# All eight triangular inverses in one chain, the last four heads in the order q, k, v, z, the input in four loads, the bias product as a whole tile, and new slots

## The chip, the cores and the metric

The kernel runs on one core of a Trainium2 chip. Its engines each work through a queue of their own in order: TensorE (PE, with its weight loads PEld), VectorE (DVE), ScalarE (ACT), GpSimd (POOL) and SyncE (SP, which only issues DMAs here). The metric is the device time of one execution, in microseconds, as a median of runs.

## What is computed

One decoder layer for 256 positions of width 1024, in float32:

```python
h = rms_norm(x, norm_w)
q_a, k_a, v_a, z_a, qkv_dn, z_dn, b_dn, a_dn = split(h @ w_in)
qa, ka = rms_norm(heads(q_a)), rms_norm(heads(k_a))     # 8 heads of 64
y_a = softmax(qa ka^T / 8 + rel_bias, causal) va * silu(z_a)
q, k, v = silu(causal_conv4(qkv_dn))                    # 4 heads of 128, q and k L2-normed
# chunks of 64: amat = I + strict(beta k k^T decay); u, w = solve(amat, ...)
o_d = delta_rule(q, k, v, decay, beta)
y_d = rms_norm(o_d) * silu(z_dn)
out = x + concat(y_a, y_d) @ w_out
```

With 256 positions the block-sparse attention has one block, so it is plain causal attention.

## The kernel before

**Products.** A float32 product is made from rounded halves: each weight chunk is copied to a high half (ScalarE, L195) and the rest (VectorE, L196), x and y likewise, and each product takes three matmuls of 256 (or 264) columns: L256 to L258 (`gemm`), L747 to L749 (`dn`), L836 to L838 (`oproj`). There are 960 of these in the program: z (gates, 96), d (delta rule's q, k, v, 288), a (attention, 384) and o (output, 192). I number them from 0 and say "product 792" for the place where o02, the first output chunk, ends. The chunks come in the order z0 to z7, d0 to d11, a (per half of the heads v, q, k, z) and o. The weights and x come by SP's queue (L183, L208): x is eight loads, one per 128 rows of the width, each followed by one z chunk.

**Order.** TensorE's order is written by hand: `products()` yields after groups of six products, and each yield is one step (`advance`). Other work of TensorE sits in generators (streams): `norm`, `gates`, `bias`, `prep0` and `prep2` (two delta-rule heads each), `heads` (norm and transpose of q and k), `pair0` to `pair3` (attention of two heads), `base` with `levels` (the triangular inverses) and `scan0` to `scan3` (the delta rule of one head). Each goes on with its next stage at the step that the table AT gives, or later if a condition in it isn't met. What a step issues stands in TensorE's queue behind the products yielded so far. The other engines are ordered by the scheduler.

**Inverses.** The 256 positions of a head are taken in two chunks of 128 (which gives the same as four of 64), so there are eight matrices of 128 by 128. `base(gq)` inverts 16 by 16 blocks of four of them by a recurrence of 15 steps with two VectorE instructions each (L507, L509); it is started after prep0 (gq 0) and after prep2 (gq 1). `levels` then joins 16 to 32, 64 and 128 by small matmuls (L529 on), each followed by a copy out of the bank on ScalarE or VectorE; when a chain is done it starts its two scans. A scan makes v (L589, L593), the state and output of its first part (L595, L596), the second part's products with the state (L610, L611), L618, L622, and then the norm, the gate (L630) and the transposes (L634), from which yh and yl (L635, L636) are made.

**Output.** OUTS gives the order of the output chunks: o02, o00, o12, o10, o03, o13, o01, o11. A chunk with second digit 2 needs heads 0 to 3 of the attention, 0 scans 0 and 1, 3 heads 4 to 7, 1 scans 2 and 3. The steps between the last product of o02 and the first of o00 hold all that is still missing for scans 0 and 1. The first split row of the output that depends on them is yl. At the end VectorE adds the residual and the result is stored.

**Bias.** Row 0 to 32 of T hold a one-hot table, `rbt` the bias values; one matmul (L381) makes the eight rows, which go by ScalarE (L384) and DRAM back into T.

Of the kernel before, what the change touches and what calls it, by code (L numbers as in the profile page):

```python
# [14 lines left out]
P = 128  # L15
# [22 lines left out]
    ("attention", 0): 88, ("attention", 1): 97, ("attention", 2): 128, ("attention", 3): 117, ("attention", 4): 120,  # L38
# [3 lines left out]
    ("base1", 8): 124, ("bias", 0): 0, ("bias", 1): 6, ("bias", 2): 43, ("gates", 0): 29, ("gates", 1): 35,  # L42
# [13 lines left out]
}  # L56
SEGS = (2, 0, 1, 3)
# [4 lines left out]
def tile_hymba_layer(ctx: ExitStack, tc: tile.TileContext, xt, wz, wdn, wat, wout, rb, cst, oneh, out):  # L62
# [81 lines left out]
    rbt = new([33, 8], "rbt")  # L144
    oht = T.rearrange("p h s -> p (h s)")[0:33, 0:384]
    POOL.memset(rbt, NEG)
    nc.gpsimd.dma_start(rbt[0:32, :], rb)
    nc.gpsimd.dma_start(oht, oneh)
    for _ in range(NWARM):
# [14 lines left out]
              + [(f"a{s}{i}", wat[4 * s + i], 1024) for hf in range(2) for s in SEGS for i in (2 * hf, 2 * hf + 1)]  # L164
# [40 lines left out]

    for k in range(KT):
        r = slice(P_COLS + k * S if k else 0, P_COLS + (k + 1) * S)
        nc.sync.dma_start(px[:, r], xt[:, r])  # L208
        load()
# [28 lines left out]
    Mts = [new([P, 4, 32], f"Mt{g}") for g in range(2)]  # L238
# [3 lines left out]
    def basis():  # L242
        for t in Mts:
            nc.gpsimd.dma_start(t, cst[:, C_ND, :])
# [178 lines left out]
    def prep(hp, n, ps):  # L423
# [50 lines left out]
        start(f"base{hp // 2}", base(hp // 2))  # L474
# [12 lines left out]
    def base(gq):  # L487
        us = slice(4 * gq, 4 * gq + 4)
        pk = rot([P, 16, 4], f"pk{gq}", "pk")
        for q in range(4):  # L490
            r = slice(32 * q, 32 * q + 32)

            DVE.scalar_tensor_tensor(out=pk[r].rearrange("p i u -> p u i"), in0=LT[r, us, 32 * q + 16:32 * q + 32],
                                     scalar=cs2[r, 0:1], in1=LT[r, us, 32 * q:32 * q + 16], op0=ALU.mult, op1=ALU.add)
        Lb = rot([P, 16, 32], f"Lb{gq}", "Lb", 1)
        DVE.transpose(Lb, pk.unsqueeze(3).to_broadcast([P, 16, 4, 8]))
        Mt = Mts[gq]
        tm = rot([P, 4, 16], f"tm{gq}", "tm")
# [4 lines left out]
        for r in range(15):  # L503
            w, nc_ = 15 - r, r // 8 + 1
            t = ap(tm, 0, (32, 2), (16, nc_), (1, w))
            m = ap(Mt, r + 1, (80, 2), (32, nc_), (1, w))
            SUB.tensor_tensor(out=t, in0=ap(Lb, 32 * (r + 1) + r, (16, 2), (0, nc_), (32, w)),  # L507
                               in1=ap(Mt, r, (80, 2), (32, nc_), (0, w)), op=ALU.mult)
            SUB.tensor_tensor(out=m, in0=m, in1=t, op=ALU.subtract)  # L509

        Mp = rot([P, 4, 4, 8], f"Mp{gq}", "Mp")
        DVE.transpose(Mp.rearrange("p u c g -> p c u g"), Mt)
        Mp = Mp.rearrange("p u c g -> p u (c g)")
        for q in range(4):
            r = slice(32 * q, 32 * q + 32)
            DVE.transpose(MT[r, us, r], Mp[r])
        yield W_BASE
        yield from levels(gq, Mp)


    def levels(gq, Mp):
# [25 lines left out]
        for q in range(2):  # L547
            POOL.tensor_copy(M[qs[q], us, qs[q]], Mp[qs[q]])
# [387 lines left out]
```

## Time and profile before

| | us |
|---|---|
| median of 3 runs | 166.14 (164.9 to 166.62) |
| profiled run | 166.0 |
| span of its trace | 164.1 |
| TensorE busy (share of the span) | 156.8 (96%) |
| VectorE busy | 130.3 (79%) |
| ScalarE busy | 103.1 (63%) |

The busy share is an average over stages. Matmuls are pipelined, so a row's duration is longer than the distance to the next row; what a matmul costs is that distance. A bracket at a row's end is the idle time before it and what ended it.

### The profile page before, as it was taken

The page shows a single profiled execution, that of the slowest core. Times are in us where ns is not written, and L with a number is a line of the kernel's source. Part 1 is how long each engine was busy: PE and PEld are TensorE (multiplying, and loading weights), DVE is VectorE, ACT ScalarE, POOL GpSimd, SP SyncE. Part 2 cuts the span into 40 slices and gives each one's busy share as a digit, 9 for nine tenths or more (in the row PEclk, how much of TensorE's full clock was granted, in tenths as well). Part 3 has the DMA queues.
Part 4 walks back from the last instruction along what each step waited for, and adds up shares of the span by engine and source line. Part 5 has one row for each costly group of instructions (what it writes and reads, how often), then busy time and mean ns, then how long its engine had stood idle before and what let it go on. Part 6 is the DMA issues. An engine that isn't in the chain of part 4 may idle for free.

```text
span 164.1 us, 4034 instructions
## 1 busy us (share of the span) xinstructions
PE 156.8 (96%) x1548; PEld 148.3 (90%) x1548; DVE 130.3 (79%) x381; ACT 103.1 (63%) x244; POOL 19.8 (12%) x29
## 2 busy tenths in 40 slices
PE   7999899999999999999999999999999979999990
PEld 7869899999999999999999989989988858999990
DVE  2569859999598999999999999987676997356261
ACT  5769497539988558787636695655657885343100
POOL 7200410000002000031230001042220010003000
PEclk9999999999999999999999999999999999999999
DMA  5999888899965327574344434434312300000033
GB/s 148 270 365 355 248 262 222 248 179 192 339 206 209 128 80 213 223 216 172 122 138 135 132 123 134 128 132 132 116 51 93 128 0 4 0 0 0 4 128 128
DMA packets 9930, 25.01 MB, mean 152 GB/s; under 512 B 1165, under 2 KB 3981, under 8 KB 9912
## 3 DMA queue, kind: packets, MB, share of 16 engines
q1 hardware_dynamic: 9208, 23.66, 46.6%
q10 hardware_dynamic: 576, 0.92, 1.5%
q8 instruction: 12, 0.20, 0.5%
q0 software_dynamic: 128, 0.18, 0.4%
q14 instruction: 6, 0.05, 0.1%
HBM read 23.52 MB, written 1.25 MB: 151 GB/s over the span
## 4 chain that ended last, share of the span: by engine, by line
PE 70%; DVE 13%; ACT 6%; DMA 3%; issue 2%; SPq 2%; POOL 1%; DVEq 0%
PE ps L256 8%; PE ps L257 7%; PE ps L258 7%; PE ps L748 6%; PE ps L749 6%; PE ps L747 6%; PE ps L836 4%; PE ps L838 4%; PE ps L837 4%; DVE wl_d L196 3%; DMA px<-xt 3%; PE ps L462 2%; DVE cv L407 2%; PE ps L689 1%; PE ps L712 1%
## 5 line engine op out<-in xcount | busy, mean ns | idle before, releaser
L256 PE MATMUL ps<-wh_a,xh 128*128 128x256 f32 x96 | 28.5, 297 | 0.0
L747 PE MATMUL ps<-xh,wh_d 128*128 128x256 f32 x96 | 27.8, 289 | 0.0
L748 PE MATMUL ps<-xl,wh_d 128*128 128x256 f32 x96 | 26.8, 280 | 0.0
L749 PE MATMUL ps<-xh,wl_d 128*128 128x256 f32 x96 | 26.8, 279 | 0.0
L257 PE MATMUL ps<-wh_a,xl 128*128 128x256 f32 x96 | 26.7, 279 | 0.0
L258 PE MATMUL ps<-wl_a,xh 128*128 128x256 f32 x96 | 26.7, 279 | 0.0
L195 ACT CAST wh_a<-wr_a 128x1024 fp32r<-128x1024 f32 x16 | 16.8, 1049 | 7.2 <-PE ps L748 3.7
L196 DVE TENSOR_TENSOR wl_a<-wr_a,wh_a 128x1024 fp32r<-128x1024 f32 x16 | 19.4, 1215 | 0.7 <-ACT wh_a L195 0.6
L256 PEld LDWEIGHTS ps<-wh_a,xh 128*128 128x128 f32 x96 | 18.1, 188 | 0.7 <-issue 0.5
L836 PE MATMUL ps<-yh,wh_o 128*128 128x256 f32 x64 | 18.7, 292 | 0.0
L257 PEld LDWEIGHTS ps<-wh_a,xl 128*128 128x128 f32 x96 | 18.1, 188 | 0.1
L258 PEld LDWEIGHTS ps<-wl_a,xh 128*128 128x128 f32 x96 | 18.1, 189 | 0.0
L748 PEld LDWEIGHTS ps<-xl,wh_d 128*128 128x128 f32 x96 | 18.1, 188 | 0.1
L747 PEld LDWEIGHTS ps<-xh,wh_d 128*128 128x128 f32 x96 | 18.0, 188 | 0.1
L407 DVE SCALAR_TENSOR_TENSOR cv<-un,px,cv 128x255 f32<-128x255 f32 (+2 forms) x36 | 16.4, 475 | 2.0 <-ACT cv L405 2.0
L749 PEld LDWEIGHTS ps<-xh,wl_d 128*128 128x128 f32 x96 | 18.0, 187 | 0.0
L837 PE MATMUL ps<-yl,wh_o 128*128 128x256 f32 x64 | 17.9, 280 | 0.0
L838 PE MATMUL ps<-yh,wl_o 128*128 128x256 f32 x64 | 17.9, 279 | 0.0
L196 DVE TENSOR_TENSOR wl_d<-wr_d,wh_d 128x1024 fp32r<-128x1024 f32 x12 | 14.6, 1214 | 1.2 <-ACT wh_d L195 1.1
L195 ACT CAST wh_d<-wr_d 128x1024 fp32r<-128x1024 f32 x12 | 12.6, 1052 | 2.4 <-PE ps L748 1.9
L196 DVE TENSOR_TENSOR wl_o<-wr_o,wh_o 128x1024 fp32r<-128x1024 f32 x8 | 9.8, 1221 | 3.6 <-ACT wh_o L195 3.6
L836 PEld LDWEIGHTS ps<-yh,wh_o 128*128 128x128 f32 x64 | 12.0, 188 | 0.5 <-issue 0.3
(210 smaller groups left out, 406.7 us busy)
## 6 DMA issues: line engine op xcount, KB each, us to landing
wr_a<-wat SPq DMA_DIRECT2D x16, 512.0 KB, 3.3
wr_d<-wdn SPq DMA_DIRECT2D x12, 512.0 KB, 5.6
wr_o<-wout SPq DMA_DIRECT2D x8, 512.0 KB, 3.3
wr_z<-wz SPq DMA_DIRECT2D x7, 260.0 KB, 5.8
T<-bd SPq DMA_DIRECT2D x8, 128.0 KB, 5.8
px<-xt SPq DMA_DIRECT2D x7, 128.0 KB, 4.9
out_t<-ot ACTq DMA_DIRECT2D x3, 256.0 KB, 2.4
cs<-cst SPq DMA_DIRECT2D x1, 192.0 KB, 4.9
```

The lines of the kernel that those rows point to most:

```text
L195: ACT.copy(h[:, r], raw[:, r])
L196: eng.tensor_tensor(out=l[:, r], in0=raw[:, r], in1=h[:, r].bitcast(F32), op=ALU.subtract)
L256: PE.matmul(ps, lhsT=xa, rhs=wh[:, cols], start=first, stop=False)
L257: PE.matmul(ps, lhsT=xb, rhs=wh[:, cols], start=False, stop=False)
L258: PE.matmul(ps, lhsT=xa, rhs=wl[:, cols], start=False, stop=last)
L407: DVE.scalar_tensor_tensor(out=a[:, 3 - j:], in0=src[:, 0:S - 3 + j], scalar=pr[:, o + j:o + j + 1], in1=a[:, 3 - j:], op0=ALU.mult, op1=A ...
L747: PE.matmul(ps, lhsT=w[0][:, wk], rhs=xh[:, k, :], start=first, stop=False)
L748: PE.matmul(ps, lhsT=w[0][:, wk], rhs=xl[:, k, :], start=False, stop=False)
L749: PE.matmul(ps, lhsT=w[1][:, wk], rhs=xh[:, k, :], start=False, stop=last)
L836: PE.matmul(ps, lhsT=w[0][:, o], rhs=yh[:, k, :], start=(first and j == 0 and (m % 2 == 0 or alone)), stop=False)
L837: PE.matmul(ps, lhsT=w[0][:, o], rhs=yl[:, k, :], start=False, stop=False)
L838: PE.matmul(ps, lhsT=w[1][:, o], rhs=yh[:, k, :], start=False, stop=(last and j == 1 and (m % 2 == 1 or alone)))
```

## The change

**Inverses.** There is one `base()` and one `levels()` for all eight, started in prep2 only. The 15 steps work on twice the width, so there are 30 VectorE instructions instead of 60; the basis tile is one `Mt` of 320 columns. `levels` takes two banks. The last copy is split: VectorE takes heads 0 and 1 (L579), ScalarE the others. All four scans are started together at the end.

**Attention.** The half for the last four heads is projected as q, k, v, z instead of v, q, k, z. **Input.** x comes in four loads of two slices. **Bias.** `rbt` and the one-hot table are parts of T, filled up to 128 rows with zeros, and the matmul writes 128 rows of 384. **Slots.** The table AT is new throughout; code lines of after are 2 or 3 higher.

```diff
-SEGS = (2, 0, 1, 3)
+SEGS = ((2, 0), (0, 0), (1, 0), (3, 0), (0, 1), (1, 1), (2, 1), (3, 1))
...
+    Tf = T.rearrange("p h s -> p (h s)")
+    oht, rbt = Tf[:, 0:384], Tf[:, 384:512]
+    POOL.memset(Tf[:, 0:512], 0.0)
...
-        nc.sync.dma_start(px[:, r], xt[:, r])
+        if k % 2 == 0:
+            r = slice(P_COLS + k * S if k else 0, P_COLS + (k + 2) * S)
+            nc.sync.dma_start(px[:, r], xt[:, r])
         load()
...
-        PE.matmul(b[0:8, :384], lhsT=rbt, rhs=oht, start=True, stop=True)
+        PE.matmul(b[:, :384], lhsT=rbt, rhs=oht, start=True, stop=True)
...
-        start(f"base{hp // 2}", base(hp // 2))
+        if hp == 2:
+            start("base", base())
...
-            t = ap(tm, 0, (32, 2), (16, nc_), (1, w))
+            t = ap(tm, 0, (32, 4), (16, nc_), (1, w))
...
-        ACT.mul(MT[0:64, us, 64:128], b64[0:64, 0], -1.0)
-        free.append(b)
-        yield W_LV
-        start(f"scan{2 * gq}", scan(2 * gq))
-        yield 1
-        start(f"scan{2 * gq + 1}", scan(2 * gq + 1))
+        DVE.tensor_scalar(out=MT[0:64, 0:4, 64:128], in0=b64[0:64, 0:4], scalar1=-1.0, scalar2=None, op0=ALU.mult)
+        ACT.mul(MT[0:64, 4:8, 64:128], b64[0:64, 4:8], -1.0)
+        free.extend((ba, bb))
+        for h in range(DH):
+            start(f"scan{h}", scan(h))
...
-        while done["vz"] < 2 + 2 * (pa // 2):
+        while (2, pa // 2) not in done or (3, pa // 2) not in done:
```

ScalarE at the start of the program, before (xh is the high half of x, sq the squares for the norm, wh_z the high half of a z chunk):

```order
L266 ACTIVATE xh<-px 128x256
L123 ACTIVATE eal<-px 128x4
L195 CAST wh_z_165<-wr_z_99 128x256
L195 CAST wh_z_165<-wr_z_99 128x264
L276 ACTIVATE sq_296<-px 128x512
L266 ACTIVATE xh<-px 128x256
L195 CAST wh_z_171<-wr_z_99 128x520
```

and of the change:

```order
L278 ACTIVATE sq_277<-px 128x512
L268 ACTIVATE xh<-px 128x256 x2
L121 ACTIVATE eal<-px 128x4
L195 CAST wh_z_160<-wr_z_99 128x256
L195 CAST wh_z_160<-wr_z_99 128x264
L195 CAST wh_z_166<-wr_z_99 128x520
```

A pass of squares and a second pass of xh now stand ahead of the first wh_z.

TensorE inside o02 (wh_o and wl_o are the halves of its weights), of the change; in before these products have only one transpose, L634 of scan 1, between them:

```order
L840 MATMUL ps_72<-yh,wl_o_1532 128x256
L578 MATMUL ps_77<-MT,X_1851 32x64 x16
L838 MATMUL ps_75<-yh,wh_o_1531 128x256
L839 MATMUL ps_75<-yl,wh_o_1531 128x256
L840 MATMUL ps_75<-yh,wl_o_1532 128x256
L838 MATMUL ps_75<-yh,wh_o_1531 128x256
L839 MATMUL ps_75<-yl,wh_o_1531 128x256
L840 MATMUL ps_75<-yh,wl_o_1532 128x256
L592 MATMUL ps_73<-vt,MT 128x128
L592 MATMUL ps_71<-vt,MT 128x128
```

The last step of the inverses (L578) and the first step of scans 0 and 1 (L592) now stand among o02's products, six products apart; L562 to L564 and L572 stand ahead of them in the same way.

TensorE between o02 and o00, before (S is a scan's state, pb the softmax weights, yd a scan's output):

```order
L838 MATMUL ps_74<-yh,wl_o_1704 128x256
L610 MATMUL ps_72<-S_1883,kq_134 128x128
L611 MATMUL ps_72<-S_1883,kq_134 128x128
L589 MATMUL ps_78<-vt,MT 128x128
```

and of the change:

```order
L840 MATMUL ps_75<-yh,wl_o_1532 128x256
L598 MATMUL ps_73<-v0d_1904,ktok 128x128
L599 MATMUL ps_73<-v_1903,aT 128x128
L598 MATMUL ps_71<-v0d_1909,ktok 128x128
L599 MATMUL ps_71<-v_1908,aT 128x128
L715 MATMUL ps_76<-cs,pb_1857 128x128 x3
L715 MATMUL ps_78<-cs,pb_1858 128x128 x3
L613 MATMUL ps_73<-S_1920,kq_130 128x128
```

In before scan 0 enters the stretch at its products with the state (L610) and scan 1 is through; after, both scans enter it at the products that make the state (L598).

## Rows read from the trace of the kernel before

**Rows 1.** Busy time by stage: us, then busy us (instructions) per engine, PEclk, DMA share, GB/s

```profile
0.00:4.05 4.05, 3.01 (x14) 3.01 (x15) 0.83 (x5) 2.18 (x4) 3.07 (x11) 1.00 0.56 146
4.05:20.30 16.25, 15.31 (x105) 13.79 (x104) 12.86 (x25) 11.91 (x22) 2.50 (x3) 1.00 0.93 310
20.30:128.93 108.63, 108.49 (x1188) 103.75 (x1187) 96.82 (x289) 76.07 (x185) 12.20 (x14) 1.00 0.54 164
128.93:137.79 8.86, 7.69 (x60) 5.62 (x59) 8.10 (x34) 7.13 (x22) 0.69 (x1) 1.00 0.15 53
137.79:160.10 22.31, 22.30 (x190) 22.09 (x188) 11.27 (x31) 5.80 (x12) 1.36 (x2) 1.00 0.07 25
```

**Rows 2.** Waits of TensorE: us in total, times, longest

```profile
PE ps L712 <- DVE pb L707: 1.2, 2, 0.9
...
PE ps L288 <- DVE sq L285: 0.5, 1, 0.5
PE ps L258 <- DVE wl_z L196: 0.4, 2, 0.2
```

**Rows 3.** Timeline, ScalarE, start: us, duration, engine line op out<-in, [idle <-releaser]

```profile
3.00 0.51 ACT L266 ACTIVATE xh<-px 128x256 fp32r<-128x256 f32 x1 [1.00 <-DMA px<-xt]
...
5.14 0.63 ACT L276 ACTIVATE sq<-px 128x512 f32<-128x512 f32 x1 [0.16 <-DMA px<-xt]
...
9.53 0.63 ACT L276 ACTIVATE sq<-px 128x512 f32<-128x512 f32 x1 [1.40 <-DMA px<-xt]
```

**Rows 4.** Timeline, TensorE, z stage: first products and the bias product

```profile
6.61 0.42 PE L258 MATMUL ps<-wl_z,xh 128*128 128x264 f32 x1
6.83 0.44 PE L256 MATMUL ps<-wh_z,xh 128*128 128x256 f32 x1
...
7.78 0.28 PE L256 MATMUL ps<-wh_z,xh 128*128 128x256 f32 x1
7.90 0.28 PE L257 MATMUL ps<-wh_z,xl 128*128 128x256 f32 x1
...
10.40 0.81 PE L381 MATMUL ps<-T,rbt 33*8 33x384 f32 x2
11.14 0.39 PE L256 MATMUL ps<-wh_z,xh 128*128 128x256 f32 x1
```

**Rows 5.** Timeline, TensorE, a place where small groups interrupt products

```profile
101.19 0.28 PE L258 MATMUL ps<-wl_a,xh 128*128 128x256 f32 x1
101.40 0.44 PE L552 MATMUL ps<-Mp,LT 32*32 32x32 f32 x16
```

**Rows 6.** Timeline, TensorE, the end of the block before o00

```profile
136.01 0.39 PE L610 MATMUL ps<-S,kq 128*128 128x128 f32 x2
...
136.45 0.38 PE L634 MATMUL ps<-cs,yd 128*128 128x128 f32 x2
136.67 0.39 PE L589 MATMUL ps<-vt,MT 128*128 128x128 f32 x2
...
137.79 0.39 PE L836 MATMUL ps<-yh,wh_o 128*128 128x256 f32 x1
```

**Rows 7.** Timeline, VectorE, two steps of the recurrence

```profile
90.84 0.20 DVE L507 TENSOR_TENSOR tm<-Lb,Mt 128x28 f32<-128x28 f32 x1
91.08 0.19 DVE L509 TENSOR_TENSOR Mt<-Mt,tm 128x28 f32<-128x28 f32 x1
```

**Rows 8.** Timeline, VectorE, in the block

```profile
130.52 1.21 DVE L196 TENSOR_TENSOR wl_o<-wr_o,wh_o 128x1024 fp32r<-128x1024 f32 x1
131.65 0.34 DVE L593 TENSOR_SCALAR v<-ps,cv 128x128 f32<-128x128 f32 x1
131.91 0.28 DVE L696 CUSTOM_DVE_ANT_0 pb<-ps,T 128x128 f32<-128x128 f32 x1
...
133.02 0.42 DVE L727 TENSOR_TENSOR ya<-ps,za 128x256 f32<-128x256 f32 x1
```

**Rows 9.** Busy time of VectorE's piece before o00

```profile
125.88:137.86 11.98, 10.81 (x85) 8.74 (x85) 11.22 (x44) 10.08 (x33) 0.69 (x1) 1.00 0.13 44
```

More of the change, by code (lines that the diff above doesn't have):

```diff
@@ L237, in tile_hymba_layer @@
     MT = new([P, 8, P], "MT")
-    Mts = [new([P, 4, 32], f"Mt{g}") for g in range(2)]
+    Mt = new([P, 320], "Mt")
     for t in (M, MT):
@@ L242, in basis @@
     def basis():
-        for t in Mts:
-            nc.gpsimd.dma_start(t, cst[:, C_ND, :])
+        for g in range(2):
+            nc.gpsimd.dma_start(Mt[:, 160 * g:160 * g + P], cst[:, C_ND, :])
     if not MTL:
@@ L526, in levels @@
         qs = q0, q1, q2, q3 = tuple(slice(32 * q, 32 * q + 32) for q in range(4))
-        for i, u in enumerate(uu):
+        a32, b32 = (b.rearrange("p (z u i) -> p z u i", z=2, i=32) for b in (ba, bb))
+        for u in range(8):
             for r in qs:
-                PE.matmul(b32[r, 2, i, 0:16], lhsT=LT[r, u, r], rhs=Mp[r, i, 0:16], start=True, stop=True)
-        X16 = rot([P, 4, 16], f"X16{gq}", "X16")
-        ACT.mul(X16, b32[:, 2, :, 0:16], cs2[:, 0:1])
+                PE.matmul(a32[r, 0, u, 0:16], lhsT=LT[r, u, r], rhs=Mp[r, u, 0:16], start=True, stop=True)
@@ L545, in levels @@
             else:
-                DVE.tensor_scalar(out=o, in0=b32[r, 3, :, 16:32], scalar1=-1.0, scalar2=None, op0=ALU.mult)
+                DVE.tensor_scalar(out=o, in0=a32[r, 1, :, 16:32], scalar1=-1.0, scalar2=None, op0=ALU.mult)
         for q in range(2):
-            POOL.tensor_copy(M[qs[q], us, qs[q]], Mp[qs[q]])
+            POOL.tensor_copy(M[qs[q], :, qs[q]], Mp[qs[q]])
         yield W_LV
-        for i, u in enumerate(uu):
+        for u in range(8):
             for r, c in ((q0, q1), (q2, q3)):
-                PE.matmul(b32[c, 0, i, :], lhsT=LT[r, u, c], rhs=Mp[r, i, :], start=True, stop=True)
@@ L553, in levels @@
-        X32 = rot([P, 4, 32], f"X32{gq}", "X32")
+                PE.matmul(b32[c, 0, u, :], lhsT=LT[r, u, c], rhs=Mp[r, u, :], start=True, stop=True)
+        X32 = rot([P, 8, 32], "X32", "X32", 1)
         ACT.copy(X32[q1], b32[q1, 0])
@@ L563, in levels @@
-        ACT.mul(MT[q0, us, q1], b32[q0, 1], -1.0)
+        for u in range(8):
+            PE.matmul(b32[q1, 1, u, :], lhsT=MT[q1, u, q1], rhs=X32[q1, u, :], start=True, stop=True)
+            PE.matmul(b32[q2, 1, u, :], lhsT=X32[q3, u, :], rhs=MT[q3, u, q3], start=True, stop=True)
+            PE.matmul(b32[q0, 1, u, :], lhsT=X32[q1, u, :], rhs=MT[q1, u, q1], start=True, stop=True)
+        DVE.tensor_scalar(out=M[q1, :, q0], in0=b32[q1, 1], scalar1=-1.0, scalar2=None, op0=ALU.mult)
+        ACT.mul(MT[q2, :, q3], b32[q2, 1], -1.0)
@@ L564, in levels @@
+        ACT.mul(MT[q0, :, q1], b32[q0, 1], -1.0)
         yield W_LV
-        b64 = b.rearrange("p (z u i) -> p z u i", z=2, i=64)
-        for i, u in enumerate(uu):
+        a64, b64 = (b.rearrange("p (u i) -> p u i", i=64) for b in (ba, bb))
+        for u in range(8):
             for c in (q2, q3):
-                PE.matmul(b64[c, 1, i, :], lhsT=LT[0:64, u, c], rhs=M[:, u, :], start=True, stop=True)
-        X64 = rot([P, 4, 64], f"X64{gq}", "k2", 4)
-        ACT.copy(X64[64:128], b64[64:128, 1])
+                PE.matmul(a64[c, u, :], lhsT=LT[0:64, u, c], rhs=M[:, u, :], start=True, stop=True)
@@ L571, in levels @@
+        X64 = rot([P, 8, 64], "X64", "k2", 4)
+        ACT.copy(X64[64:128], a64[64:128])
         yield W_LV
-        for i, u in enumerate(uu):
+        for u in range(8):
             for c, o in ((q0, 0), (q1, 32)):
-                PE.matmul(b64[c, 0, i, :], lhsT=X64[64:128, i, o:o + 32], rhs=MT[64:128, u, 64:128], start=True, stop=True)
-        ACT.mul(MT[0:64, us, 64:128], b64[0:64, 0], -1.0)
-        free.append(b)
-        yield W_LV
-        start(f"scan{2 * gq}", scan(2 * gq))
-        yield 1
@@ L785, in products @@
         n = 20
[L786 removed]
+        for seg, hf in SEGS:
             cols = slice(hf * S, (hf + 1) * S)
[L788 to L820 removed]
@@ new lines, in products @@
+            ps = yield from grab1()
+            for i in range(2):
+                w = chunk(n)
+                n += 1
+                for j in range(4):
+                    k = 4 * i + j
+                    for c in range(2):
+                        first, last = k == 0 and c == 0, k == KT - 1 and c == 1
+                        if seg == 3:
+                            dn(ps[:, c * S:(c + 1) * S], w, slice(j * S + c * P, j * S + (c + 1) * P), k, first, last)
+                        else:
+                            gemm(ps[:, c * S:(c + 1) * S], (xh, xl), w, k, c, slice(j * S, (j + 1) * S), first, last)
+                    yield
@@ new lines, in products @@
+            if seg < 2:
+                start(f"heads{seg}{hf}", heads4(seg, hf, ps))
+            elif seg == 2:
+                for c in range(2):
+                    ACT.mul(V[:, c, cols], ps[:, c * S:(c + 1) * S], rhalf[:, c:c + 1])
+                free.append(ps)
+            else:
+                if not za:
+                    za.append(rot([P, 4, S], "za", "Lb", 1))
+                zs = rot([P, 2, S], f"zs{hf}", "k2", 4)
+                DVE.tensor_tensor(out=zs, in0=two(ps), in1=rbc.unsqueeze(1).to_broadcast([P, 2, S]), op=ALU.mult)
+                free.append(ps)
+                ez = rot([P, 2, S], f"ez{hf}", "k2", 4)
+                act(ez, zs, AF.Tanh, scale=0.5)
+                DVE.scalar_tensor_tensor(out=za[0][:, 2 * hf:2 * hf + 2, :], in0=ez, scalar=1.0, in1=zs, op0=ALU.add,
+                                         op1=ALU.mult)
@@ L822, in products @@
+            done[seg, hf] = 1
         po, ot = {}, {}
```

111 lines of the change are left out of this document (37 added, 74 removed), and 29 rows, old and new, of the table AT.

## The prediction

> **What bounds the kernel now.** I read the page's busy shares first, then the waits of TensorE, then busy time by stage, then the timelines of the places that the change touches. The stage table [rows 1] cuts the span (164.1 us; the profiled run took 166.0, so 1.9 lie outside the span, and the median of the runs is 166.14) at the first d product, at the end of o02 and at the start of o00. From 20.30 to 128.93 TensorE is busy for 108.49 of 108.63 us: whatever is saved on another engine there is worth nothing by itself. The z stage loses 0.94 of 16.25 us, with the DMA engines at a share of 0.93 and 310 GB/s. The stretch between o02 and o00 (I call it the block) loses 1.17 of 8.86, and there VectorE is the full engine (8.10). Behind o00 TensorE is full again, and what is left from 160.10 to the end, 4.0 us, is the residual and the store. The waits of TensorE [rows 2] say the same: softmax normalisation in the block 1.2 us, the wl_z splits 0.4, the sum of squares 0.5. The granted clock is 1.00 (the 2.4 GHz level) in every stage. So only four things can move the time: the z stage, what TensorE itself has to do, the block, and new waits.
>
> **The z stage.** The first x load is now 256 columns longer, and ScalarE does one sum-of-squares pass and two xh passes before the first wh_z. In before xh starts at 3.00 and a pass of 512 columns takes 0.63 (its successor starts 0.54 later) [rows 3]. So 0.54 for the pass and 0.42 for the second xh come ahead of wh_z, and the 128 KB more of the first load take 0.42 at the 310 GB/s of the z stage, 0.9 at the 146 of the stage before (estimates from [rows 1]); I take 0.42, since by then all engines of the DMA run. The first product moves from 4.05 to about 5.4, +1.4. Against that: ScalarE idles 1.40 us for an x load before its second pass [rows 3], the waits for wl_z and sq (0.9) are likely to fall away since TensorE comes later to the same data, and the bias product with its 0.74 (10.40 to 11.14 [rows 4]) leaves the stage. It comes back in full behind product 108: it still streams 384 columns, in two passes, and that the tile is now 128 by 128 instead of 33 by 8 does not shorten or lengthen a stream (bounds: 0.4, if the cold neighbours on both sides cost it, to 1.0). The rest of the late start I count as half given back (0.5), because the waits of [rows 2] in this stage show that data, and not only its own rate, holds TensorE up there. Sum up to d0: +1.4 − 0.9 − 0.74 − 0.5 = −0.74, so d0 near 19.6 for 20.30; then +0.74 for the bias product: 0 net. Bounds: −1.4 (the late start is given back whole and the longer load costs nothing) and +1.1 (of the late start only 0.3 is given back).
>
> On the four loads: the row shows the DMA engines at 0.93 of their time [rows 1], and the bytes stay the same, so fewer issues alone bring nothing. The Trainium skill (DMA: Bandwidth & Descriptors, Rules for kernel authors) says that many small transfers should be coalesced into a large one; by that rule this stage would gain, which is the first rival's way, with the time given there.
>
> **TensorE's own work from d0 to the end of o02.** Two rows of a z product stand 0.12 apart (7.78, 7.90) [rows 4]. Where a small group interrupts the weight products, the neighbour takes 0.21 (101.19 to 101.40) and often the one behind too [rows 5]: 0.14 to 0.2 per place. In before the products are interrupted in 43 places up to the end, after in 34 (up to o02's end 36 and 27, counted in the two orders). Nine fewer: −1.5 (bounds −1.2 and −1.8).
> Then work moves from ahead of o02's end to behind it: the first products of scan 0 and of scan 1 with the state (L595 with L596) and scan 1's L610 with L611, 0.44 each (136.01 to 136.45 [rows 6]), make 1.3, and scan 1's L618, L622, L634 and one L589, at most 0.22 each (136.45 to 136.67 [rows 6]), I count as 0.6. So −1.9 here, to be paid later.
> VectorE's recurrence halves from 60 to 30 instructions of about 0.20 that stand 0.24 apart [rows 7] (twice the width costs little: 28 elements took 0.20, and 128 took 0.26 for L593, 131.65 to 131.91 [rows 8]): 5 to 7 us of VectorE saved, worth 0 here, since TensorE hides it; the cover is the products between prep2 and slot 122.
> New waits: the g chain must now be ready at product 162, in before at 204. By rate that is 19.6 + 0.74 + 66 × 0.117 = 28.1 us. In before 42 products more, 4.9 us, lay ahead of it, without a wait; how early it could have been ready the rows don't show, so 0 to 1 us of wait. The steps of the inverse chain in o02 stand six products (0.70) apart, and an evacuation of 256 to 512 columns takes 0.35 to 0.5 (0.42 for the 256 columns of L727 [rows 8]) plus the end of the matmul before it, so each of four steps may wait 0 to 0.3. Together I take +0.5 (bounds 0 and +1.5).
> So o02 ends at 128.93 − 1.5 − 1.9 + 0.5 = 126.0.
>
> **The block.** In before VectorE works through 44 instructions in 11.98 us, from 125.88 to the last split before o00 [rows 9], nearly without a gap (11.22 busy). After, the piece from the L579 copy (which needs L578) to the split of scan 1's output has 45: it loses eight of a pair's softmax (131.91 to 133.02 for eight, 1.1 [rows 8]), a wl_o (130.52 to 131.65, 1.13 [rows 8]) and the za product (0.57, half a split, as it has half the columns), and gains six small ones (two L607, L596, L626, two L633; 0.28 each, near L593's 0.26), L628 (0.1), a ya product and the L579 copy (0.35 each, a little under the 0.42 of L727, which overlaps its successor): −2.8 + 2.48 = −0.32, about −0.35. So 11.6 us. L578 ends two six-product steps and four small matmuls ahead of o02's end, near 124.1. o00 begins at about 135.8, in before at 137.79 [rows 6]: −2.0. Bounds: 10.9 us (VectorE never idles, against 0.76 idle before) and 13.2 (each latency of the two scans' steps added one behind the other).
>
> **Behind o00.** The state products and the S products of both remaining scans now lie behind o00, in before of one: 2 × 0.44 = +0.9 at [rows 6]'s price. TensorE is full there (22.30 of 22.31 [rows 1]), so it counts. The tail of 4.0 us is the same.
>
> **Sum.** 0 − 1.5 − 1.9 + 0.5 = −2.9 up to o02's end; the block takes 9.8 instead of 8.86, +0.9; behind it +0.9. Together −1.1 on 166.0: **164.9 us**, 0.7% under the median. What a measurement of this kernel can tell from no change is about 1%, 1.7 us.
>
> **Rivals.**
> A, faster. The z stage gains too: larger loads bring x for k = 1 and 3 earlier, where ScalarE idled 1.40 us [rows 3], and the waits of [rows 2] go: −1.2; and VectorE never idles in the block, 10.9 for 11.6: −0.7. 163.0. For it: the share of 0.93. Against it: the first product is later by more than a microsecond.
> B, slower. The chain L564, L572, L578, L592 and then both scans is bound by latency: one chain for all eight inverses means that no scan can start before all are done, with only 24 products (2.8 us) as cover. If the block takes 13.2 (+1.6) and the chain's steps wait 1.5 more, 168.0. For it: in before scan 1 was through by o02, and TensorE waited 0.91 once in the block even so [rows 2]. Against it: two scans side by side cover each other. It decides from the point where o00 starts: later than 137.0 the kernel is slower than before, later than 138.6 by over 1%.
> C, no gain. TensorE idles about a microsecond between the warm-up products and the first product, and the first products stay 0.22 apart (6.61, 6.83 [rows 4]) for longer; in before 13 of them did so. Another 13 at 0.10 more each are +1.3: 166.2, or 167 to 168 where x for k = 2 is late as well. The Trainium skill (TensorE: Matmul & The Clock Gate, What's actually happening) calls the throttled state the default that activity releases; that would let an idle stretch cost time, by this rival's 166.2. The granted clock in [rows 1] reads 1.00 in this stage, so the trace of before does not show it in that column.
>
> **Chances.** The forecast 0.48 (0.25 of it under 164.5, the rest within 1%), A 0.22, B 0.18 (0.04 within 1%, 0.14 slower), C 0.12 (0.08 within 1%, 0.04 slower). Faster by over 1%: 0.47; within 1%: 0.35; slower: 0.18. The forecast's own range is 163.6 to 166.3; the whole range goes from A's middle less half its width (162.4) to B's case without its chain waits and with the z stage's upper bound (164.9 + 1.6 + 1.1 = 167.6).
>
> **What would show it.** First product near 5.4, first d product near 19.6, and the bias product 0.74 long behind product 108. TensorE without waits from d0 to slot 122; o02's end near 126.0; waits on L564, L572 and L578 under 0.3 each. Recurrence steps of 0.20 to 0.22, thirty of them, and VectorE's total down to about 124. o00 at 135.8, out of a block in which VectorE is busy nine tenths. The prediction is wrong if o02's end comes after 127 (the places weren't worth their price, or the g chain makes TensorE wait), or if the block takes over 11 us with VectorE idle in it (B).

## The result and the profile after

The changed kernel is slightly slower: 166.81 us (median of 20 runs, 165.17 to 173.27) against 165.34 us (20 runs, 164.60 to 166.62), a ratio of 1.0054 with a 95% interval of 1.0031 to 1.0077. The ratio, like all that follow, leaves out seven of the changed kernel's runs, which took 167.7 to 173.3 us, six of them at a mean granted clock of 0.95 to 0.99; of the kernel before none had to go. The forecast was 164.9 us, 0.7% faster. The profiled execution has a span of 165.2 us, 1.1 more than before.

Busy time by stage of the changed kernel, with the columns of [rows 1]; the cuts are the first product, the first d product, the last step of the inverse chain ahead of o02, the end of o02, the start of o00 and the end of the products:

```profile
5.42:19.53 14.11, 13.18 (x100) 12.40 (x101) 12.56 (x26) 11.30 (x20) 1.50 (x1) 1.00 0.96 344
19.53:120.09 100.56, 97.90 (x1024) 95.13 (x1022) 85.57 (x219) 66.08 (x154) 12.30 (x11) 1.00 0.61 176
120.09:127.46 7.37, 7.37 (x149) 6.42 (x148) 5.96 (x20) 5.81 (x17) 0.00 (x0) 1.00 0.22 74
127.46:138.03 10.57, 9.32 (x70) 6.99 (x69) 8.59 (x37) 7.28 (x24) 1.44 (x2) 1.00 0.00 0
138.03:161.62 23.59, 23.45 (x199) 23.05 (x197) 12.09 (x34) 7.32 (x17) 1.36 (x2) 1.00 0.06 24
```

The d0 product comes at 19.53 (before 20.30), o02 ends at 127.46 (128.93), o00 starts at 138.03 (137.79). So 1.47 us in hand at the end of o02 are lost, and more, in the block, which takes 10.57 us for 8.86. From 19.53 to 120.09 TensorE is idle for 2.66 us, where before it was idle for 0.14. The waits of TensorE, which [rows 2] answer to, name them:

```profile
PE ps L258 <- ACT wh_z L195: 1.6, 2, 1.0
PE ps L556 <- issue: 1.1, 1, 1.1
...
PE ps L666 <- DVE qn L658: 0.8, 1, 0.8
PE ps L440 <- ACT kq L121: 0.8, 1, 0.8
PE ps L625 <- ACT v L623: 0.8, 2, 0.5
PE ps L715 <- DVE pb L710: 0.5, 2, 0.3
```

L556 (a step of `levels`), L666 (transposes of q) and L440 (transposes of prep0) are new, 1.08 + 0.82 + 0.76 = 2.66 us. "issue" says that the engine waited for nothing that the profile shows. The timeline of TensorE at that wait:

```profile
116.71 0.28 PE L752 MATMUL ps<-xh,wl_a 128*128 128x256 f32 x1
116.91 0.56 PE L556 MATMUL ps<-Mp,LT 32*32 32x32 f32 x23
118.55 0.32 PE L556 MATMUL ps<-Mp,LT 32*32 32x32 f32 x9 [1.08 <-issue]
```

It stands in the middle of one group: 23 rows of the group's 32 have run, nine are left, and in the program only the group's first matmul waits for a semaphore.

The other lines that the forecast spoke of: the bias product, TensorE behind product 108,

```profile
20.95 0.81 PE L383 MATMUL ps<-T 128*128 128x384 f32 x2
21.30 0.57 PE L750 MATMUL ps<-xh,wh_d 128*128 128x256 f32 x1
```

takes 0.35 us to its successor, where [rows 4] have 0.74; the successor is 0.41 ahead of its own, so that the two together take 0.76 for 0.96 before. At its new place it thus costs 0.64 (0.76 less one product of 0.12). The 0.74 of before is not its price there, as the prediction read it. It is mostly a wait: the weight load of the successor waits for wh_z, whose copy on ScalarE ends at 11.08, and the successor starts at 11.14.

```profile
11.13 0.19 PEld L256 LDWEIGHTS ps<-wh_z,xh 128*128 128x128 f32 x1 [0.65 <-ACT wh_z L195]
```

The rows of the products hide this wait, because the bias product's row of 0.81 us covers it.

The recurrence, groups of VectorE by line (busy time, mean ns of one), has half the instructions, each a little longer:

```profile
L509 DVE TENSOR_TENSOR tm<-Lb,Mt 128x56 f32<-128x56 f32 (+10 forms) x15 | 3.3, 220 | 0.2
L511 DVE TENSOR_TENSOR Mt<-Mt,tm 128x56 f32<-128x56 f32 (+10 forms) x15 | 2.9, 196 | 0.2
```

And the piece of VectorE from the first copy behind L578 (L579) to the split of scan 1's output, which [rows 9] answer to:

```profile
125.60:138.85 13.25, 11.92 (x88) 9.26 (x87) 10.89 (x46) 9.29 (x32) 1.44 (x2) 1.00 0.00 1
```

13.25 us, with VectorE busy for 10.89 of them; before, 11.22 of 11.98.

### The profile page after: what moved, and what is told of

Same layout as the page of the kernel before. It is cut to its first block, busy times and chain, and to the rows that moved or that the text cites. A ratio compares the mean times of both kernels' runs of the same rounds, so it can differ in the third digit from the quotient of the medians.

```text
span 165.2 us, 3984 instructions
## 1 busy us (share of the span) xinstructions
PE 154.6 (94%) x1548; PEld 147.0 (89%) x1548; DVE 126.3 (76%) x338; ACT 100.9 (61%) x236; POOL 21.1 (13%) x28
## 4 chain that ended last, share of the span: by engine, by line
PE 54%; DVE 15%; DMA 13%; ACT 7%; issue 3%; POOL 3%; SPq 2%; DVEq 0%; ACTq 0%; POOLq 0%
DMA wr_d<-wdn 9%; PE ps L258 5%; PE ps L259 5%; PE ps L260 5%; PE ps L838 5%; PE ps L839 5%; PE ps L840 4%; DMA px<-xt 4%; PE ps L750 3%; DVE wl_d L196 3%; PE ps L751 3%; PE ps L752 3%; DVE cv L409 2%; PE ps L692 2%; POOL r L133 2%
## 5 line engine op out<-in xcount | busy, mean ns | idle before, releaser
L258 PE MATMUL ps<-wh_a,xh 128*128 128x256 f32 x96 | 27.7, 288 | 0.0
L409 DVE SCALAR_TENSOR_TENSOR cv<-un,px,cv 128x255 f32<-128x255 f32 (+2 forms) x36 | 15.8, 477 | 0.1
L195 ACT CAST wh_o<-wr_o 128x1024 fp32r<-128x1024 f32 x8 | 8.4, 1047 | 7.3 <-PE ps L839 3.1
```

Source lines behind the costliest of these rows:

```text
L195: ACT.copy(h[:, r], raw[:, r])
L258: PE.matmul(ps, lhsT=xa, rhs=wh[:, cols], start=first, stop=False)
L409: DVE.scalar_tensor_tensor(out=a[:, 3 - j:], in0=src[:, 0:S - 3 + j], scalar=pr[:, o + j:o + j + 1], in1=a[:, 3 - j:], op0=ALU.mult, op1=A ...
```

## The experiments

Ratios are to the kernel before, measured beside each kernel on its chip; e1 to e4, e5 to e8, e9 to e11 and the last two ran together.

**The changed kernel again.**

> The changed kernel itself, to be compared with the next three on one chip. Theory 1 (three new waits of TensorE, at L440, L556 and L666, 2.66 us together, took the gain): the same three waits are seen again, 0.6 to 1.1 us each, and the ratio to the kernel before is 1.002 to 1.010. Rival (the waits were chance in one execution): they are elsewhere or gone.

Measured: 165.98 us, 1.0042 (1.0008 to 1.0077). In its profile the wait at L666 is 0.8 and the one at L556 0.7 us; the one at L440 is not there. So two of the three belong to the kernel, and the third did not come in this execution.

The z stage differs too, though the kernel is the same. The first products stand 0.21 to 0.22 apart until 9.29 and 0.12 apart from there; in the profile after they are 0.12 apart from the fourth row (6.17) on:

```profile
9.08 0.41 PE L259 MATMUL ps<-wh_z,xl 128*128 128x256 f32 x1
9.29 0.36 PE L260 MATMUL ps<-wl_z,xh 128*128 128x256 f32 x1
9.49 0.28 PE L258 MATMUL ps<-wh_z,xh 128*128 128x264 f32 x1
9.61 0.29 PE L259 MATMUL ps<-wh_z,xl 128*128 128x264 f32 x1
```

So d0 comes at 20.08 (19.53 in the profile after, 20.30 before) and product 120 at 23.55 (23.00 and 23.57). A spacing of 0.21 is that of products at a granted clock of 0.50 (e4 below). The clock column reads 1.00 all the same: the first clock record of this trace lies at 9.44 us (4.71 in the profile after, 6.96 in before), and a stretch without a record counts as 1.00. In the four profiles with the changed kernel's z stage (after, e1, e3, e4) d0 lies at 19.53, 20.08, 20.44 and 19.27, so one profile can't price this stage to better than a microsecond.

**A shift of TensorE's stream.**

```diff
+    for _ in range(16):
+        PE.matmul(psum[7][0:32, 0:16], lhsT=ones[0:32, 0:32], rhs=ones[0:32, 0:16], start=True, stop=True)
```

> Changed kernel with sixteen tiny matmuls (32 by 32, 16 columns) behind the warm-up products, where TensorE is idle for 1.0 us anyway; they only shift every later instruction in TensorE's stream. The stall at L556 stands in the middle of 32 matmuls of which only the first waits for data. Theory 1a (TensorE runs dry of instructions there, since 64 + 96 + 32 small matmuls in bursts use the stream up faster than it is fetched): the stall of 1.08 us at L556 moves or vanishes, 0.7 to 1.1 us less than the changed kernel. Rival 1b (it waits for copies of VectorE, ScalarE or GpSimd): the stall stays at the same matmul with 0.9 to 1.2 us, no change in time.

Measured: 165.25 us, 0.9992 (0.9966 to 1.0017), 0.73 us under e1. No wait at L556's step; one of 0.24 us, again "issue", stands in the middle of the step before (L539 and L541 in the changed kernel). The price is that the first product comes at 6.14 us, and still the kernel gains. Of the 0.9 us by which the profiled span is shorter than e1's, the stall makes 0.47; 0.44 lie ahead of d0 (19.64 for 20.08), and whether the tiny matmuls or chance brought those isn't shown.

**Later slots for the two transposes.**

```diff
-("prep0", 2): 55, ("prep0", 4): 57, ("prep0", 5): 59, ("prep0", 6): 60, ("prep0", 7): 61, ("heads00", 1): 92
+("prep0", 2): 57, ("prep0", 4): 59, ("prep0", 5): 61, ("prep0", 6): 62, ("prep0", 7): 63, ("heads00", 1): 95
```

> Changed kernel with the second transposes of prep0 (L440) and what follows them two steps later, and the first q transposes (L666) three steps later, so that VectorE and ScalarE are ready when TensorE comes there. Theory 1 (these waits reach the end of the kernel): the waits of 0.76 and 0.82 us go and the time falls by 1.2 to 1.6 us. Rival 2 (the work that is bound by VectorE in the block sets the end and takes up what is won ahead of it): under 0.5 us.

Measured: 165.13 us, 0.9981 (0.9948 to 1.0013), 0.85 us under e1. Both waits are gone; the stall at L556 stands at 1.3 us. As e1 had no wait at L440, the gain of the runs is about the 0.8 of L666. The profiles can't confirm it: here d0 is 0.36 later and the stall 0.6 longer than in e1, and the span only 0.2 shorter.

**The chain three slots earlier.**

```diff
-("base", 2): 127, ("base", 3): 128, ("base", 4): 129, ("base", 5): 130, ("base", 6): 131
+("base", 2): 124, ("base", 3): 125, ("base", 4): 126, ("base", 5): 127, ("base", 6): 128
+("scan0", 0): 129 ... ("scan0", 5): 134, scan1 the same; ("scan2", 0): 136, ("scan3", 0): 136
```

> Changed kernel with the five later steps of the inverse chain 3 slots earlier (18 products, 2.1 us) and scans 0 and 1 one slot apart from there on, so that most of both scans lies among the last products of a and among o02's. Theory 3 (the block is long because both scans enter it from their first step, a matter of the slots): the block between o02 and o00 falls from 10.6 to 7 or 8.5 us and the time by 2 to 4 us. Rival 3b (VectorE's work sets the block, wherever the chain stands): the block keeps 10 us and the time changes by under 0.7 us. Rival 3c (six products are too short a cover for a step of the chain): waits of 0.5 us and more at L556, L562, L572 and L578 that give back what the block loses.

Measured: 176.07 us, 1.0664 (1.0623 to 1.0705): much slower, which no theory had. TensorE waits 1.4 us at L562, as rival 3c said, and 3.2 at L637. But the larger loss is another. Busy time by stretch; the last three columns are granted clock, DMA share and GB/s:

```profile
112.00:116.00 4.00, 3.09 (x125) 2.68 (x113) 2.04 (x5) 1.95 (x4) 0.77 (x2) 1.00 0.12 48
116.00:118.00 2.00, 1.56 (x52) 1.50 (x53) 0.80 (x2) 0.31 (x1) 0.00 (x0) 0.74 0.42 131
118.00:126.00 8.00, 8.00 (x84) 7.21 (x84) 0.42 (x1) 1.98 (x5) 0.00 (x0) 0.50 0.10 37
126.00:128.00 2.00, 1.97 (x12) 1.76 (x11) 1.38 (x2) 1.77 (x4) 0.00 (x0) 0.70 0.00 0
```

Behind small matmuls of 32 rows, few products and the wait of 1.4 us, the granted clock falls to 0.50, the 1.2 GHz level, for more than 8 us. The rows of products there stand 0.21 apart instead of 0.12. The block itself falls from 10.57 to 5.52 us (135.10 to 140.62), below even theory 3's range, but o02 ends 7.6 us later than in the profile after. So whether the chain's lateness costs time can't be read from this run.

**Both edits, shift and slots.**

> Changed kernel with both the sixteen tiny matmuls behind the warm-up and the later slots of L440 and L666. Theory 1 (the three waits of TensorE add up and all reach the end): about 1.6 us less than the changed kernel, ratio to the kernel before 0.990 to 0.996, none of the waits at L440, L556, L666. Rival 2 (the block takes up what is won ahead of it): as with one of the two edits, 0.997 to 1.001.

Measured: 164.37 us, 0.9933 (0.9900 to 0.9965), 1.61 us under e1: the gains of the two (0.73 and 0.85) add up. None of the three waits is left:

```profile
PE ps L150 <- DVE ones L137: 1.0, 1, 1.0
PE ps L627 <- ACT v L625: 0.7, 2, 0.5
PE ps L262 <- DVE wl_z L198: 0.5, 2, 0.3
PE ps L717 <- DVE pb L712: 0.5, 2, 0.3
```

The block has not moved by a hundredth, though it starts 3.56 us earlier than in the profile after (columns as above; 10.57 us from the end of o02 to o00):

```profile
123.90:134.47 10.57, 9.32 (x70) 6.99 (x69) 8.59 (x37) 7.27 (x24) 1.44 (x2) 1.00 0.01 2
```

This kernel beats the kernel before and the changed one, and its ratio is the one that the forecast gave to the changed kernel (164.9 to 166.0, 0.9934). Its profiled run (163.51 us) is one of its two fastest, so its profile flatters it against that of before.

**Single parts, put into the kernel before.** The four loads alone:

```diff
-        r = slice(P_COLS + k * S if k else 0, P_COLS + (k + 1) * S)
-        nc.sync.dma_start(px[:, r], xt[:, r])
+        if k % 2 == 0:
+            r = slice(P_COLS + k * S if k else 0, P_COLS + (k + 2) * S)
+            nc.sync.dma_start(px[:, r], xt[:, r])
```

> Kernel before with the input in four loads, nothing else. Theory 4 (the z stage wins from the loads what it won in the changed kernel): first product near 5.4 us and first d product 0.2 to 0.8 us earlier than 20.30; since TensorE hardly waits from there to the block, the same 0.2 to 0.8 us at the end, ratio 0.995 to 0.999. Rival 4b (the late first product costs what the fewer waits win): d0 at 20.2 to 20.9, ratio 0.999 to 1.004.

Measured: 171.20 us, 1.0329 (1.0284 to 1.0374). The first product comes at 5.48, d0 at 20.48, inside rival 4b's range: no gain up to there. But the first products stand 0.21 to 0.22 apart until 9.6 us here, so after what e1 showed this one profile doesn't settle the loads. The loss comes later, in new waits at steps of the inverse chain (0.8 us at L530, 1.0 at L553, 1.9 at L559), behind which the clock falls again:

```profile
106.00:108.00 2.00, 0.37 (x24) 0.34 (x24) 1.52 (x2) 1.41 (x2) 0.00 (x0) 1.00 0.00 0
108.00:110.00 2.00, 2.00 (x21) 1.99 (x13) 1.83 (x3) 0.53 (x2) 0.00 (x0) 0.70 0.73 260
110.00:112.00 2.00, 2.00 (x18) 1.78 (x19) 0.44 (x2) 0.00 (x0) 1.38 (x1) 0.50 0.63 154
```

With the loads the scheduler also gives VectorE and ScalarE another order in places far behind the loads, while TensorE's slots stay; that this is what makes TensorE wait is argued, not shown.

The bias product as a whole tile alone:

```diff
-        PE.matmul(b[0:8, :384], lhsT=rbt, rhs=oht, start=True, stop=True)
+        PE.matmul(b[:, :384], lhsT=rbt, rhs=oht, start=True, stop=True)
```

> Kernel before with the bias product as a whole tile (128 rows and columns, zeros filled in), at its old place. It prices the tile: in before the narrow product stood 0.74 us ahead of its successor, in the changed kernel the whole one 0.35. Theory 5 (the shape is what costs): 0.30 to 0.45 us to the next row at the old place and about 0.4 us less there. Rival 5b (the place is what costs, beside products that are waiting for data): 0.6 to 0.8 us as before. The time changes by under 0.4 us with either, since the z stage waits for data right behind it.

Measured: 166.57 us, 1.0057 (1.0024 to 1.0089). The product stands 0.35 us ahead of its successor at the old place too. That would be theory 5, but the data differ as well: the copy of wh_z that the successor needs ends at 10.88 here, 0.65 us ahead of the bias product (11.53), and in before at 11.08, 0.7 us behind its start (10.40). So there was a wait for data in before and none here, which is rival 5b's reason, and the run doesn't show that the shape costs anything. d0 comes at 19.85 for 20.30, within the spread of that stage. The time is no better, with a wait of 0.5 us at L439 that the kernel before doesn't have; why it is worse by 0.6% isn't settled.

The inverse chain alone (order of the projections, input, bias and attention's slots as before; the diff is that of `base` and `levels` in the change, with the change's slots for them and the scans):

> Kernel before with only the inverses in one chain, with the changed kernel's slots for the chain and the scans; the projections keep the order v, q, k, z, input and bias are as before, the attention keeps its old slots, so that by the conditions the pairs 2 and 3 come behind the start of o00 and the stretch before o00 holds hardly more than scans 0 and 1. Theory 6 (latency: from L578 to o00 the steps of the two scans come one behind the other): that stretch still takes 10 to 12 us from the copy of L578's result. Rival 6b (VectorE's work sets it): without the softmax of two heads and a pair's gate, some 3.5 us of VectorE, it falls to 8 to 9.5 us. Time: by theory 6, 166.5 to 169; by 6b, 164 to 166.

Measured: 183.64 us, 1.1065 (1.1006 to 1.1124), with waits of 4.7 us in front of the transposes of the scans' output, 2.5 in front of transposes of k or q, and the clock down again. The time shows only that the slots of the rest don't fit. What the run does tell is the stretch from the copy of L578's result to o00, in which there are nearly only the two scans:

```profile
129.94:140.80 10.86, 7.28 (x47) 5.76 (x45) 6.97 (x28) 4.92 (x14) 1.36 (x2) 0.97 0.00 0
```

10.86 us with VectorE busy for 6.97. In the changed kernel the same stretch (125.60 to 138.03) is 12.43. With the work of two heads taken out, rival 6b wanted 9.5 us at most. The scans' steps one behind the other take most of the block, theory 6; the attention beside them adds some 1.6 us. The clock of 0.97 makes the 10.86 a little too long.

**o12 ahead of o00, on the kernel with shift and slots.**

```diff
-OUTS = ((0, 2), (0, 0), (1, 2), (1, 0), (0, 3), (1, 3), (0, 1), (1, 1))
+OUTS = ((0, 2), (1, 2), (0, 0), (1, 0), (0, 3), (1, 3), (0, 1), (1, 1))
-("pair3", 0): 136, ("pair3", 1): 138, ("pair3", 2): 140
+("pair3", 0): 138, ("pair3", 1): 141, ("pair3", 2): 144
```

(The scans' slots from the second products on go with it.)

> The kernel with the pad and the later slots (0.9933 of before), but with the output chunk o12, which needs only heads 0 to 3, ahead of o00, so that its 24 products (2.8 us) lie between the steps of scans 0 and 1, and the attention of heads 6 and 7 behind the start of o00, where TensorE is full. Theory 6 (latency of the scans' steps sets the stretch to o00, and TensorE idles in it): o00 starts 0.5 to 1.5 us after where it does with o00 first, with 24 products more done, and the time falls by 1 to 2.5 us, ratio 0.978 to 0.988. Rival 6b (VectorE's work sets it): the softmax of heads 6 and 7 is gone from the stretch, so o00 would start 3 us earlier, and the time would fall by 3 us and more, below 0.978. Rival 7 (scans 2 and 3 start later and then make TensorE wait in front of o01): waits of over 1 us at L627 or L639 behind o00, no gain, 0.990 to 1.000.

Measured: 168.18 us, 1.0171 (1.0114 to 1.0229). o00 starts at 133.44, 1.0 us earlier than in e5 and with o12's 24 products done. That lies between theory 6 (0.5 to 1.5 later) and rival 6b (3 earlier): TensorE had room for the products in the block, and without the softmax of heads 6 and 7 the stretch from o02's end to o00 still takes 8.74 us (124.70 to 133.44) for 10.57. So the scans' steps make most of it, and the attention some 1.8, near the 1.6 of e8. But TensorE then waits 1.08 us for yl behind o00's first product, and the clock falls to 0.94 and 0.50 in the two stretches of 2 us from 134 on. At product 888 this kernel is at 152.85, e5 at 149.11. All that was won is lost behind o00, where the attention of heads 6 and 7 and the late scans 2 and 3 now stand.

**Eight loads again, on the kernel with shift and slots** (the reverse of the diff of e6):

> The kernel with the pad and the later slots, but with the input in eight loads again: what the four loads are worth in the changed kernel. Theory 4 (they win at the first d product, as 19.5 to 20.1 us against 20.30 of before suggests): first product at 4.05, first d product 0.2 to 0.7 us later than with four loads, ratio 0.995 to 0.999. Rival 4b (the late first product costs what they win): the same within 0.3 us, 0.992 to 0.995. Rival 8 (the order that the scheduler gives the other engines changes with the loads and no longer fits the slots): new waits behind d0, ratio over 1.000.

Measured: 164.89 us, 0.9969 (0.9939 to 0.9999). The first product does not come at 4.05, since the sixteen tiny matmuls hold TensorE until 6.14 here, so the run prices the loads only in part. d0 is at 20.92. e9, with four loads and its first product at 6.14 as well, has d0 at 20.18. But these 0.74 us are not the loads': the first products stand 0.21 to 0.22 apart until 9.34 in e9 and until 11.94 in e10, and 0.12 behind that; some twelve rows more at 0.10 more each are 1.2 us. The interval also overlaps that of e5 (0.9900 to 0.9965). Theory 4 is not shown, and what the four loads are worth stays open.

**The chain one slot earlier, on the kernel with shift and slots.**

```diff
-("base", 2): 127 ... ("base", 6): 131, ("scan0", 0): 132, ("scan1", 0): 132
+("base", 2): 126 ... ("base", 6): 130, ("scan0", 0): 131, ("scan1", 0): 131
```

> The kernel with the pad and the later slots, with the last five steps of the inverse chain and the first steps of scans 0 and 1 one slot earlier (six products, 0.7 us). Theory 3 (the lateness of the chain counts): o00 starts 0.4 to 0.7 us earlier and the time falls by as much, 0.988 to 0.991. Rival 3b (VectorE or the steps of the attention set o00's start): under 0.2 us, 0.992 to 0.995. Rival 3c (the granted clock falls as with the chain three slots earlier, where it was 0.50 to 0.78 from 115 to 130 us): a stretch with a clock under 0.9 behind the chain, and 1 us and more lost, over 1.000.

Measured: 168.42 us, 1.0176 (1.0129 to 1.0223). Rival 3c: TensorE waits 1.3 us at L600 and 1.5 at L717 for VectorE, and then the clock falls:

```profile
134.00:136.00 2.00, 0.52 (x6) 0.26 (x3) 2.00 (x13) 1.31 (x6) 0.71 (x2) 1.00 0.00 0
136.00:138.00 2.00, 1.90 (x10) 1.18 (x12) 1.67 (x7) 1.27 (x3) 0.71 (x1) 0.90 0.03 8
138.00:140.00 2.00, 2.00 (x12) 1.41 (x10) 0.91 (x2) 0.12 (x2) 0.00 (x0) 0.50 0.00 0
```

And the stall with "issue" is back, but now among the large products between two steps of the chain:

```profile
114.26 0.28 PE L754 MATMUL ps<-xh,wl_a 128*128 128x256 f32 x1
115.48 0.28 PE L752 MATMUL ps<-xh,wh_a 128*128 128x256 f32 x1 [0.94 <-issue]
```

A product needs nothing from the chain. So I counted how many matmuls had run when TensorE stopped. Busy time from the start to each stall (second entry: TensorE's busy time and, in brackets, its matmuls), in the order changed kernel, e11, e8:

```profile
0.00:118.54 118.54, 112.90 (x1117) 109.23 (x1118) 98.84 (x246) 79.41 (x177) 18.30 (x24) 1.00 0.66 197
```

```profile
0.00:115.47 115.47, 112.43 (x1117) 109.07 (x1118) 98.36 (x246) 79.13 (x177) 20.00 (x24) 1.00 0.67 198
```

```profile
0.00:122.09 122.09, 116.02 (x1117) 111.37 (x1117) 98.85 (x246) 80.75 (x178) 15.49 (x23) 0.99 0.62 190
```

It is 1117 each time, and also in e1, e2, e3 and the two that follow: eight profiles of seven kernels (e1 is the changed kernel itself), with and without tiny matmuls ahead, at two different steps and at a product. The stall goes with the place in TensorE's stream and not with what stands there: theory 1a.

The traces also have what arrives just before. A DMA queue of the kind "instruction" brings twelve blocks of 16 KB in every execution. In the eight profiles with the stall, TensorE goes on 1.22 to 1.48 us after the eighth block has landed (117.34 and 118.55 in the profile after). In the other seven it runs its 1118th matmul 1.81 to 4.01 us after that landing (111.38 and 113.58 in e5) and does not stop there. This is what theory 1a wants: where TensorE comes there too early, it stands until the block is in. It is read from the times of 15 profiles; no run moves that block by itself.

**Half the shift, and L666's slot alone.**

```diff
-    for _ in range(16):
+    for _ in range(8):
```

> As the kernel with the pad and the later slots, but with eight tiny matmuls instead of sixteen; the sixteen ran to 5.5 us in one execution and held the first product up to 6.14 us in others. Theory 1a (the stall is a matter of the place in TensorE's stream; a shift by half as much still moves the bursts off it): no stall of over 0.3 us at L556's line, first product at 5.3 to 5.5 us, 0.1 to 0.6 us less than with sixteen, ratio 0.989 to 0.993. Rival (the shift is too small): a stall of 0.5 us or more among the small matmuls again, 0.995 to 0.999.

Measured: 164.35 us, 0.9932 (0.9907 to 0.9957): the same as with sixteen. The first product comes at 5.52, and a stall of 0.42 us is left at the 1117th matmul, so I missed by a little: a shorter shift takes away more than half of the stall and not all.

```diff
-("heads00", 1): 92
+("heads00", 1): 95
```

> As before it, with eight tiny matmuls, but of the slots only that of the first q transposes (L666) is later; the second transposes of prep0 (L440) stay where the change put them. It tells the two waits apart. If the wait at L440 is part of the kernel (0.76 us in one execution, none in the second): 0.3 to 0.8 us more than with both slots, ratio 0.993 to 0.997. If it was chance of that execution: the same as with both within 0.2 us, 0.988 to 0.993.

Measured: 164.44 us, 0.9933 (0.9901 to 0.9964): the same as with both slots. In its profile there is no wait at L440, though its slots are those of the change, as there is none in e1, e2 and e4. The 0.76 us of L440 in the profile after were chance of that execution.

## Why the prediction was wrong

**Step by step.** By the differences to the profiled execution of before, which at 166.0 us was itself 0.7 above that kernel's median; the second column of measurements is e1, the changed kernel's other profile:

| step | forecast | profile after | e1 |
|---|---|---|---|
| z stage with the bias product (product 120) | 0 | −0.57 | −0.02 |
| fewer places, work moved behind o02 (what is left of o02's end) | −3.4 | −3.56 | −3.94 |
| new waits up to o02's end, as recorded | +0.5 (0 to 1.5) | +2.66 | +1.53 |
| block, o02's end to o00 | +0.9 | +1.71 | +1.71 |
| behind o00, to the end of the products | +0.9 | +1.28 | +1.28 |
| residual and store | 0 | −0.48 | −0.48 |
| sum | −1.1 | +1.0 | +0.1 |

**The step that failed** is "New waits: … Together I take +0.5 (bounds 0 and +1.5)". I looked for waits where the order had become tighter, at the g chain and at the steps of the inverse chain in o02, and there is none at either (L562 to L564, L572 and L578 have no recorded wait). The waits came where I had not looked. At L666 the slot of the first transposes of q is 92 instead of 96, and they wait for VectorE's norm, which itself waits 0.81 us for GpSimd's power (2.55 us). I had read in the list of slots that it moved and had not followed its chain. The stall at the 1117th matmul is no semaphore's and stands in no order; I had priced the bursts of small matmuls by their number alone. L440's wait belongs to that one execution.

The recorded waits are even too small, since a row's duration hides the start of a wait. From product 120 to the end of o02 TensorE takes 105.36 us in before, 104.46 in the profile after, 102.96 in e1 and 100.77 in e5, which has none of the three. So the waits cost 3.7 in the profile after and 2.2 in e1, and fewer places and moved work brought −4.6 where the sum has −3.4.

e5 undoes the waits and lands on the forecast's ratio. That it lands just there is luck: places and moved work came out 1.2 better than forecast, the block and the work behind o00 1.2 worse, and the sum has 0.5 for waits that e5 doesn't have.

**The block.** From L579 to the last split I forecast 11.6 us of VectorE without a gap, bounds 10.9 and 13.2; it takes 13.25 with VectorE idle for 2.36 of it. The sum of instructions was about right (10.89 busy; 46 instructions, where the forecast's own list gives 43 and its text 45), the bound was not: rival B's reason, the latency of the scans' steps, holds in the block (e8: 10.86 us with hardly anything beside the scans, e9: 24 products more fit in). B's price for it (13.2) was right. Its other half, waits at L562, L572 and L578, did not come, and o00 starts at 138.03, 1.0 us past the point that B named as decisive for slower; in e1 it starts at 137.07.

**What was right.** The first product (5.42, forecast 5.4); the recurrence's cost (6.2 us in 30 steps for 10.8 in 60) and that it is worth nothing at the end; that fewer places and moved work count; that work behind o00 counts in full, though it was 1.28 instead of 0.9.

**Right by luck: the z stage.** d0 came at 19.53, forecast 19.6, but not by the forecast's terms. The waits that were to fall away are 0.90 us of this stage in the profile after (0.59 and 0.31), as they were 0.94 in before; what was won is that only the first three products stood over 0.2 apart, where in before it was about 13. In e1 it was 18, and d0 came at 20.08. The bias product's −0.74 was a misread wait, and behind product 108 it costs 0.64. Rival A's mechanism, that larger loads take the waits of this stage away, isn't shown.

**Rival C** is half there: its longer stretch of wide spacing did not come in the profile after, where products stand 0.12 apart from the fourth on (6.17, 6.29), but it did in e1 and e3, some five rows more than in before and not 13. The 1.00 that the prediction read in [rows 1] doesn't speak against it, as the first clock record of before lies at 6.96. The Trainium skill (TensorE: Matmul & The Clock Gate, What's actually happening) calls the slow state the default that activity releases. The wide spacing at the start and the fall of the clock in e4, e6, e9 and e11 behind waits agree with that; in the changed kernel's profile the column stays at 1.00.

**Open** stay why the kernel with the tile of the bias alone is 0.6% slower, what the four loads are worth, and which part of the shift's gain lies in the z stage. That TensorE lacks instructions at the 1117th matmul is read from the times of the blocks, not from a run that moves them.

## What to carry to other kernels

A change that makes one engine's work cheaper and sets all slots anew is won or lost in the waits that the new slots make: go through each group that moved to an earlier place on the engine that never waits, and follow back what it needs, not only through the chain that the change is about. A stretch between two dependent stages is priced by its longest chain of steps as well as by the sum of its busiest engine; here it took more than the chain nearly alone (12.43 us, 10.86 in e8). Before a stage is priced from one profile, look at how much it moves between profiles of the same code, and look at the waits of the weight loads besides those of the products. Parts of a change that were fitted together can't be tried one by one in the old kernel when a scheduler gives the other engines a new order with each edit: the single parts here cost 0.6% to 10.6%, the whole 0.5%.

## What the runs showed of the hardware

- TensorE stops for 0.24 to 1.32 us at the same place of its stream, the 1117th matmul, in seven kernels with dense groups of 32-row matmuls (11 ns apart) ahead of it, and goes on 1.22 to 1.48 us after the eighth 16 KB block of an instruction queue has landed; the kernel before, with 1120 matmuls at 113.50 us, does not stop. A few tiny matmuls at the program's start shift the dense groups against that place; kernels with them were 0.5% faster (e2 to e1, e5 to e3), not all of it from the stall.
- Waits of 1.1 to 1.9 us of TensorE, with small matmuls around them, were followed by a granted clock of 0.50 (1.2 GHz) for 3.4 us in e6, e9 and e11 and for 10.2 us in e4, so that a wait cost more than its length. In the changed kernel's profile, with a longest wait of 1.08 us behind d0, the column shows no fall; e9's wait was as long, so the length of the wait alone doesn't decide.
- The first products of the program stand 0.21 to 0.22 apart, as at a granted clock of 0.50 in e4, and then 0.12. The change came at 6.17, 9.49, 10.38 and 6.19 us in four profiles with the same z stage (after, e1, e3, e4), and moved d0 by up to 1.2 us.
- A wait can stand at the weight load and not at the product: 0.65 us in before behind the bias product (0.74 us to its successor), where the products' rows show none. The three waits of the profile after are 2.66 us in the products' rows, and the stretch that they stand in is 3.7 us longer than in e5.
